# Residual stores on ScalarE's queue, half of the gating product on GpSimd, and the first four MLP units through the common raw ring

## The chip, the cores and the metric

The kernel runs on one core of one Trainium2 chip. The metric is the device time of one launch in microseconds (us), as the median of several runs. Engines are called PE (TensorE, the matrix engine), DVE (VectorE), ACT (ScalarE), POOL (GpSimd) and SP (SyncE, which here only issues transfers).

## The reference

A two-layer backbone over 512 latent tokens and 256 context tokens of width 1024, in float32. Layer 0 mixes tokens by neighbourhood attention beside spatial gating, layer 1 by retention; each layer then has a gated MLP with a depthwise convolution over three tokens. Around every sub-layer stands a sandwich of norms:

```python
x = x + g1 * rmsnorm(y_lat, norm_g[i, 1])
h = modulate(rmsnorm(x, norm_g[i, 2]), sh2, sc2)
x = x + g2 * rmsnorm(conv_ffn(h, ...), norm_g[i, 3])

def conv_ffn(h, w_in, conv_w, conv_b, w_out):
    a = dwconv3(h @ w_in, conv_w, conv_b)      # w_in: 1024 x 5632
    gate, up = jnp.split(a, 2, axis=-1)
    return (jax.nn.silu(gate) * up) @ w_out
```

Layer 0 does this for the latent and the context tokens, layer 1 for the latent tokens alone.

## The kernel before, in words

**Tiles.** Tokens stand in tiles of 128: tiles 0 to 3 are latent, 4 and 5 context. Every matmul is done as three (lines 94, 95, 96) on operands that were split into a high and a low part: ACT copies a 128x1024 unit of weights to its high part (line 68), DVE subtracts that from the raw unit to get the low part (line 69).

**The end of each sub-layer.** Four times in the kernel a mixer or an MLP ends token tile by token tile: after attention (tiles with names ending in b, output `ysg`), after the first MLP (c, `fin` and `yf`), after retention (d, `yr`) and after the last MLP (e, `yf`). For each token tile PE makes the two 512-wide halves of y, DVE adds them up (line 494), and `residual` (from line 316) follows: ACT sums the squares of each half (line 292), DVE multiplies each half by the gate (line 324), POOL makes one over the root mean square in two small instructions (lines 297 and 278), DVE multiplies by it and adds the residual x (line 327), ACT sums squares of the new x, POOL makes its root, the new x is stored to `xd` in DRAM, and the normed x is written in halves by DVE (line 336) and ACT (line 337). There are 6, 6, 4 and 4 such token tiles, 20 in all. In the last of the four the output is stored instead, and the second norm is left out, so `xd` is stored for 16. PE then transposes the normed tiles (line 407 before an MLP, 359 before retention) into the next sub-layer's operand.

**The opening of an MLP.** `plain` (from line 1373) computes the first two features, j = 0 and 1, each from a gate unit (i = 0) and an up unit (i = 1): four units of weights in the order (j, i) = (0,0), (0,1), (1,0), (1,1), called `wp00`, `wp10`, `wp01` and `wp11` in the trace (`wp{i}{j}`; in layer 0 the fourth is `wpm`), loaded as `f{l}{i}{j}r`: `f010r` is layer 0, i = 1, j = 0. Each unit is multiplied first with the operand's first half of columns (`pf`, from the blocks called `hb`), and later, when the last token tiles are through, with the second half (`pf...b`). The later features j = 2 to 21 use another scheme with seven products and are PE's steady work.

**Rings and pools.** Raw units are loaded by SP into a ring of three buffers, `raw`, in a pool that lives through the whole kernel. Up units (i = 1) go to a single buffer of their own, `rawu`, which lies in the MLP's own pool, as do the convolution taps `cw` and some of the split units (in layer 1, all of `wp10`, `wp01`, `wp11`). That pool is opened where the mixer's pool has ended.

**Order.** The code is not run in the order in which it is written: a planner fixes each engine's order when the kernel is built, from its own estimates of durations, the memory that is free and the order of the code. On the chip each engine then goes through its list in that order and waits where an operand is late. All transfers but a few sit on SP's list (line 54).

Of the kernel before, what the change touches and what calls it, by code (L numbers as in the profile page):

```python
# [13 lines left out]
ALU = mybir.AluOpType  # L14
AX = mybir.AxisListType

P = 128
# [23 lines left out]
class Trunk:  # L41
# [274 lines left out]
    def residual(self, t, y, gate, src, last, name, xt):  # L316

        V = self.V
        self.load(xt, src)
        hv = [slice(0, 512), slice(512, 1024)]  # L320
        for n, h in enumerate(hv):
            self.ssq(y[:, h], f"y{name}{t}", n)
        for h in hv:
            V.tensor_tensor(out=y[:, h], in0=y[:, h], in1=gate[:, h], op=ALU.mult)
        r = self.rms(f"y{name}{t}")
        for n, h in enumerate(hv):
            V.scalar_tensor_tensor(out=xt[:, h], in0=y[:, h], scalar=r, in1=xt[:, h], op0=ALU.mult, op1=ALU.add)
            if last:
                self.load(self.out[t * P : (t + 1) * P, h], xt[:, h])
            else:  # L330
                self.ssq(xt[:, h], f"x{name}{t}", n)
        if last:
            return
        self.load(self.xd[t], xt)
        r = self.rms(f"x{name}{t}")
        V.tensor_scalar(out=y[:, hv[0]], in0=xt[:, hv[0]], scalar1=r, scalar2=None, op0=ALU.mult)
        self.S.activation(y[:, hv[1]], xt[:, hv[1]], AF.Copy, scale=r)
# [882 lines left out]
    def ffn(self, l, y, final, gates=None):  # L1220
# [4 lines left out]
        S, V, T, G, a = self.S, self.V, self.T, self.G, self.a  # L1225
# [8 lines left out]
        with ExitStack() as ctx:  # L1234
            fp = self.phase(ctx, f"ffnp{l}", 0)
            cw = fp.tile([P, 44, 4], F32, name=f"cw{l}", tag="cw")
            self.load(cw, a["conv_col"][:, l * 176 : l * 176 + 176])
            if not first:
                for tag in ("rawu", "wh5", "wl5", "wh6", "wl6", "pre0", "pre1"):
                    fp.tile([P, 1024], F32R if tag[0] == "w" else F32, name=f"at{tag}", tag=tag, bufs=1)  # L1240
# [17 lines left out]
            def slot(kind, name):  # L1258

                h = homes[kind][ring[kind] % len(homes[kind])]  # L1260
                ring[kind] += 1
                i = int(h[1])
                if h[0] == "w":
                    pool = self.bp if i < 3 else fp
                    return [pool.tile([P, 1024], F32R, name=f"{name}{x}", tag=f"w{x}{i}", bufs=1) for x in "hl"]
                pool = self.bp if i < 4 else self.lp
                return [pool.tile([P, 1024], F32R, name=f"{name}{x}", tag=f"y{i + m}", bufs=1) for m, x in enumerate("hl")]

            def raw(src, name, up=False):
                if up:  # L1270
                    t = fp.tile([P, 1024], F32, name=f"{name}r", tag="rawu", bufs=1)
                else:
                    t = self.bp.tile([P, 1024], F32, name=f"{name}r", tag="raw", bufs=3)
                self.load(t, src)
                return t

            def win(j, i):
                r = (l * 44 + (j, NF + j)[i]) * P
                return raw(a["ffn_in"][r : r + P], f"f{l}{i}{j}", i == 1)

            H = [slice(0, 512), slice(512, 1024)]
            halves = lambda u: [[x[:, h] for x in u] for h in H]
# [1 line left out]
            def product(ps, w, b, kind):  # L1284


                for k in range(4):
                    self.mm3(
                        ps,
                        [x[:, k * P : (k + 1) * P] for x in w],  # L1290
                        b(k),
                        k == 0 and kind in ("only", "open"),
                        k == 3 and kind != "open",
                        kind == "onto",
                    )
# [4 lines left out]
            def take(pre, i, half, ps, scale=1.0):  # L1300
                for c, b, w in cuts[half]:
                    S.activation(pre[:, i, c : c + w], ps[:, b : b + w], AF.Copy, scale=scale)  # L1302
# [6 lines left out]
            def conv(j, pre):  # L1309
                cv = fp.tile([P, 2, W], F32, name=f"cv{l}{j}", tag="cv", bufs=1)  # L1310
                for i, f in enumerate((j, NF + j)):
                    w0, w1, w2, b = (cw[:, f, m : m + 1] for m in range(4))
                    d, s = cv[:, i, :], pre[:, i, :]
                    S.activation(d, s, AF.Identity, scale=w1, bias=b)  # L1314
                    V.scalar_tensor_tensor(  # L1315
                        out=d[:, 1:W], in0=s[:, 0 : W - 1], scalar=w0, in1=d[:, 1:W], op0=ALU.mult, op1=ALU.add
                    )
                    V.scalar_tensor_tensor(  # L1318
                        out=d[:, 0 : W - 1], in0=s[:, 1:W], scalar=w2, in1=d[:, 0 : W - 1], op0=ALU.mult, op1=ALU.add
                    )  # L1320
                S.activation(cv[:, 0], cv[:, 0], AF.Silu)  # L1321
                V.tensor_tensor(out=cv[:, 0], in0=cv[:, 0], in1=cv[:, 1], op=ALU.mult)  # L1322
                if first and j == NF - 1:
                    g = fp.tile([P, 2, W], F32R, name=f"g{l}{j}", tag="pre0")
                    g = [g[:, 0], g[:, 1]]
                else:
                    g = [fp.tile([P, W], F32R, name=f"g{l}{i}{j}", tag=f"g{i}", bufs=ng) for i in range(2)]
                self.split(g[0], g[1], cv[:, 0])
                return g
# [43 lines left out]
            def plain(js, steps):  # L1373
                d, ps = {}, {}
                for j in js:
                    for i in range(2):
                        if not first and (j, i) == (js[0], 0):
                            u = self.wp
                            ring["o"] += 1
                        elif first and (j, i) == (js[1], 1):  # L1380
                            u = None
                        elif first:
                            u = slot("i", f"wp{i}{j}")
                        else:
                            if (j, i) == (js[1], 1):
                                ring["i"] = 3
                            u = slot("i" if (j, i) == (js[1], 1) else "o", f"wp{i}{j}")
                        if first or u is not self.wp:
                            r = win(j, i)
                            if u is None:  # L1390
                                t = [
                                    fp.tile([P, 2, 512], F32R, name="wpm0", tag="yp"),
                                    self.bp.tile([P, 2, 512], F32R, name="wpm1", tag="G0", bufs=1),
                                ]
                                d[j, i] = [[t[m][:, x] for x in range(2)] for m in range(2)]
                                for m in range(2):
                                    self.split(*d[j, i][m], r[:, H[m]])
                                continue
                            self.split(u[0], u[1], r)
                        d[j, i] = halves(u)  # L1400
                ring["i"] = 0
                self.need(0)
                order = [(j, i) for j in js for i in range(2)]
                for x, (j, i) in enumerate(order):
                    if x == 3:
                        self.need(1)
                    ps[j, i] = [self.ps(f"pf{l}{i}{j}", "A", (P, n))]
                    product(ps[j, i][0], d[j, i][0], hb(11), "open")
                    product(ps[j, i][0], d[j, i][1], hb(21), "close")
                sums = self.block_sums(l)  # L1410
                for j in js:
                    for i in range(2):
                        p = self.ps(f"pf{l}{i}{j}b", "CB"[j], (P, n))
                        ps[j, i].append(p)
                        product(p, d[j, i][0], h12, "open")
                        product(p, d[j, i][1], hb(22), "close")
                        for half in range(2):
                            take(pres[j % len(pres)], i, half, ps[j, i][half])
                    if j == js[0]:
                        steps[0]()  # L1420
                    next(sums, None)
                    gs[j] = conv(j, pres[j % len(pres)])
                    steps[1 + j]()
                for _ in sums:
                    pass
                steps[3]()
# [48 lines left out]
            LAST = NF - 2 * GF  # L1475
            nxt, steps = weights(2)
            plain((0, 1), steps)
            for j in range(2, NF):
                d = nxt
# [45 lines left out]
            if first:  # L1525
# [10 lines left out]
                xt = [fin[:, 4], fin[:, 5], fin[:, 8]]  # L1536
            else:
                fin = fp.tile([P, 4, D], F32, name="fin", tag="blk")
                xt = [fin[:, i] for i in range(4)]
# [193 lines left out]
```

## Time and profile before

| | us |
|---|---|
| median of the runs (1898.76 to 1901.52) | 1898.84 |
| the profiled execution's own time | 1893.99 |
| its span, first to last instruction | 1892.2 |
| PE busy in it | 1800.1 |
| DVE busy | 1402.8 |
| ACT busy | 1029.2 |
| POOL busy | 325.8 |

Rows from the trace give a start in us from the span's beginning, a duration, the engine, the line of the kernel, the operation, and output<-input. What stands in brackets at the end is the idle time of the engine before the row and what ended it. SPq is SP's transfer list. L12 is line 12.

### The profile page before, as it was taken

The numbers are of one execution on the slowest core, as the hardware profiler recorded it, in microseconds if no ns is written. First come the engines' busy times: TensorE is split into PE (matmuls) and PEld (weight loads), VectorE is DVE, ScalarE is ACT, GpSimd is POOL, SyncE is SP. The second block draws the span as 40 slices with busy tenths as digits, with TensorE's granted clock in tenths as the row PEclk, the third lists the DMA queues.
The fourth block names the chain that finished last, engine by engine and source line by source line (L and its number), as shares of the span: only waits on it lengthen the run. The fifth ranks groups of instructions, "written<-read, shape, count | busy, mean of one in ns | idle before, by whom it ended". The sixth has DMA issues, their size and how long they took to land. (4 is left out here: it accounts for less than half of the span.)

```text
span 1892.2 us, 28751 instructions
## 1 busy us (share of the span) xinstructions
PE 1800.1 (95%) x10928; PEld 1591.7 (84%) x10928; DVE 1402.8 (74%) x2352; ACT 1029.2 (54%) x1857; POOL 325.8 (17%) x446
## 2 busy tenths in 40 slices
PE   7998989979999999999989999999999989999998
PEld 4886867669889899998879889988989779889996
DVE  4844788679877778777877666675665689989877
ACT  6533545666555555555565434434444377666763
POOL 1102122130122222222121010011011100222221
PEclk9999999999999999999989999999999989999999
DMA  7333332132577877776744313322421225878772
GB/s 290 115 100 106 93 101 79 57 136 76 175 176 156 184 158 167 145 169 135 232 146 131 119 52 112 112 95 62 134 66 48 100 81 148 212 188 195 178 162 99
DMA packets 83823, 250.32 MB, mean 132 GB/s; under 512 B 10578, under 2 KB 12114, under 8 KB 83684
## 3 DMA queue, kind: packets, MB, share of 16 engines
q1 hardware_dynamic: 58436, 200.72, 32.8%
q0 software_dynamic: 25248, 47.75, 15.2%
q8 instruction: 86, 1.41, 0.3%
q14 instruction: 53, 0.43, 0.1%
HBM read 191.81 MB, written 39.85 MB: 122 GB/s over the span
## 5 line engine op out<-in xcount | busy, mean ns | idle before, releaser
L214 DVE SCALAR_TENSOR_TENSOR acc<-ar,cs,acc 128x512 f32<-128x512 f32 x256 | 189.5, 758 | 35.5 <-DMA ar<-in_adaw 19.7
L1463 POOL DMA_DIRECT2D yf<-yp x64 | 55.9, 873 | 260.2 <-ACT yp L1459 229.2
L1314 ACT ACTIVATE cv<-pre,cw 128x770 f32<-128x770 f32 (+1 forms) x88 | 80.9, 923 | 27.2 <-DVE pre L1307 25.9
L1315 DVE SCALAR_TENSOR_TENSOR cv<-pre,cw,cv 128x769 f32<-128x769 f32 (+1 forms) x88 | 77.2, 880 | 7.2 <-ACT cv L1314 7.2
L1459 ACT COPY yp<-wf 128x512 f32<-128x512 f32 x118 | 67.9, 577 | 18.1 <-PE wf L96 18.0
L1318 DVE SCALAR_TENSOR_TENSOR cv<-pre,cw,cv 128x769 f32<-128x769 f32 (+1 forms) x88 | 77.2, 881 | 0.7
L1302 ACT ACTIVATE pre<-px 128x256 f32<-128x256 f32 (+2 forms) x160 | 54.3, 367 | 41.8 <-PE px L93 33.6
L1098 POOL TENSOR_SCALAR rrr<-rmv 128x2 f32<-128x2 f32 x16 | 3.1, 193 | 363.2 <-DVE rmv L1095 363.2
L1463 POOL DMA_DIRECT2D yd<-ypg x48 | 42.1, 903 | 132.1 <-ACT ypg L1459 130.6
L1463 POOL DMA_DIRECT2D yd<-yp x48 | 42.6, 902 | 126.7 <-ACT yp L1459 126.6
L68 ACT ACTIVATE g<-cv 128x770 fp32r<-128x770 f32 (+1 forms) x44 | 32.5, 738 | 32.6 <-DVE cv L1322 32.4
L93 PE MATMUL px<-hs,wd 128*128 128x384 f32 x240 | 45.4, 337 | 0.0
L93 PEld LDWEIGHTS px<-hs,wd 128*128 128x128 f32 x240 | 42.3, 188 | 1.9 <-DVE pre L1307 0.4
L1307 DVE TENSOR_TENSOR pre<-pre,pz 128x256 f32<-128x256 f32 (+1 forms) x60 | 20.8, 371 | 29.2 <-PE pz L96 29.1
L69 DVE TENSOR_TENSOR g<-cv,g 128x770 fp32r<-128x770 f32 (+1 forms) x44 | 36.1, 821 | 7.4 <-ACT g L68 7.3
L1302 ACT ACTIVATE pre<-py 128x384 f32<-128x384 f32 (+1 forms) x40 | 17.5, 437 | 43.9 <-DVE cv L1318 25.6
L1322 DVE TENSOR_TENSOR cv<-cv 128x770 f32<-128x770 f32 (+1 forms) x44 | 36.2, 822 | 4.3 <-ACT cv L1321 3.1
L1321 ACT ACTIVATE cv<-cv 128x770 f32<-128x770 f32 (+1 forms) x44 | 32.7, 742 | 11.7 <-DVE cv L1318 11.6
L1078 DVE SCALAR_TENSOR_TENSOR of<-rx,e,of 128x256 f32<-128x256 f32 x64 | 28.9, 477 | 8.4 <-PE rx L96 7.9
L869 ACT ACTIVATE sc<-sc,sst 128x512 f32<-128x512 f32 x32 | 23.0, 719 | 22.1 <-DVE sc L860 21.6
L1459 ACT COPY ypg<-wf 128x512 f32<-128x512 f32 x54 | 30.7, 578 | 6.5 <-PE wf L96 6.4
L205 POOL MEMSET acc<- 128x512 f32 x32 | 19.1, 600 | 84.5 <-DVE al L69 62.2
(2985 smaller groups left out, 7181.1 us busy)
## 6 DMA issues: line engine op xcount, KB each, us to landing
ar<-in_adaw SPq DMA_DIRECT2D x96, 512.0 KB
yf<-yp POOLq DMA_DIRECT2D x64, 256.0 KB, 4.2
yd<-yp POOLq DMA_DIRECT2D x54, 256.0 KB, 5.2
yd<-ypg POOLq DMA_DIRECT2D x54, 256.0 KB, 5.0
fin<-xd SPq DMA_DIRECT2D x10, 512.0 KB
xd<-xd SPq DMA_DIRECT2D x8, 512.0 KB
xn<-in_x SPq DMA_DIRECT2D x6, 512.0 KB
xb<-in_x SPq DMA_DIRECT2D x6, 512.0 KB
```

The lines of the kernel that those rows point to most:

```text
L68: self.S.activation(hi, src, AF.Copy)
L69: self.V.tensor_tensor(out=lo, in0=src, in1=hi.bitcast(F32), op=ALU.subtract)
L93: mm = lambda *p, **k: self.nc.tensor.matmul(*p, skip_group_check=True, **k)
L214: V.scalar_tensor_tensor(out=acc[s], in0=raw[:, kk * 512 : kk * 512 + 512], scalar=self.cs[:, 8 * s + k : 8 * s + k + 1], in1=acc[s], op0= ...
L1302: S.activation(pre[:, i, c : c + w], ps[:, b : b + w], AF.Copy, scale=scale)
L1314: S.activation(d, s, AF.Identity, scale=w1, bias=b)
L1315: V.scalar_tensor_tensor(out=d[:, 1:W], in0=s[:, 0 : W - 1], scalar=w0, in1=d[:, 1:W], op0=ALU.mult, op1=ALU.add)
L1318: V.scalar_tensor_tensor(out=d[:, 0 : W - 1], in0=s[:, 1:W], scalar=w2, in1=d[:, 0 : W - 1], op0=ALU.mult, op1=ALU.add)
L1321: S.activation(cv[:, 0], cv[:, 0], AF.Silu)
L1322: V.tensor_tensor(out=cv[:, 0], in0=cv[:, 0], in1=cv[:, 1], op=ALU.mult)
L1459: S.copy(v, ps)
L1463: G.dma_start((yd[t] if first else y[t])[:, o], v, accum_op=ALU.add)
```

## The change

Four edits. In `residual`, the first half of y times gate goes to POOL and only the second half stays on DVE; and the store of the new x to `xd` is issued by ACT instead of SP. In the MLP, the up units of the features j = 0 and 1 are loaded into the common ring `raw` instead of `rawu`, so that all four units of `plain` go through it; and the load of the taps `cw` is moved from the beginning of the MLP to behind the four units.

```diff
@@ residual
-        for h in hv:
-            V.tensor_tensor(out=y[:, h], in0=y[:, h], in1=gate[:, h], op=ALU.mult)
+        for E, h in zip((self.G, V), hv):
+            E.tensor_tensor(out=y[:, h], in0=y[:, h], in1=gate[:, h], op=ALU.mult)
...
-        self.load(self.xd[t], xt)
+        self.S.dma_start(self.xd[t], xt)
@@ ffn
             cw = fp.tile([P, 44, 4], F32, name=f"cw{l}", tag="cw")
-            self.load(cw, a["conv_col"][:, l * 176 : l * 176 + 176])
...
             def win(j, i):
                 r = (l * 44 + (j, NF + j)[i]) * P
-                return raw(a["ffn_in"][r : r + P], f"f{l}{i}{j}", i == 1)
+                return raw(a["ffn_in"][r : r + P], f"f{l}{i}{j}", i == 1 and j > 1)
...
                 ring["i"] = 0
+                self.load(cw, a["conv_col"][:, l * 176 : l * 176 + 176])
                 self.need(0)
```

## Rows read from the trace of the kernel before

**Rows 1.** The page's head: the span, and busy us by engine.

```profile
span 1892.2 us, 28751 instructions
PE 1800.1 (95%) x10928; PEld 1591.7 (84%) x10928; DVE 1402.8 (74%) x2352; ACT 1029.2 (54%) x1857; POOL 325.8 (17%) x446
```

**Rows 2.** Stages: window, its us, busy us (count) of PE, PEld, DVE, ACT, POOL; PEclk.

```profile
409.00:432.50 23.50, 13.96 (x59) 12.09 (x60) 19.82 (x31) 17.31 (x36) 5.67 (x9) 0.72 0.34 117
432.50:460.00 27.50, 27.50 (x157) 27.50 (x157) 25.10 (x31) 16.90 (x28) 0.00 (x0) 0.99 0.20 58
...
500.00:930.00 430.00, 421.61 (x2184) 387.70 (x2183) 342.09 (x488) 246.99 (x425) 101.36 (x131) 1.00 0.74 165
935.00:985.00 50.00, 43.36 (x215) 35.83 (x214) 38.85 (x61) 30.51 (x72) 16.01 (x23) 0.90 0.41 148
...
1522.40:1532.20 9.80, 2.03 (x9) 1.57 (x8) 7.27 (x14) 6.08 (x15) 2.63 (x4) 0.65 0.37 121
1532.20:1560.00 27.80, 27.39 (x214) 26.73 (x215) 24.73 (x40) 19.90 (x37) 0.00 (x0) 0.94 0.25 75
...
1883.00:1892.20 9.20, 0.00 (x0) 0.00 (x0) 3.41 (x6) 1.44 (x4) 1.36 (x2) 0.73 0.26 98
```

**Rows 3.** PE's waits from 408.5 to 434: us in total, times, longest.

```profile
PE ht L407 <- DVE ysg L336: 4.2, 1, 4.2
PE pf L94 <- ACT wp00h L68: 2.2, 1, 2.2
```

**Rows 4.** PE's waits from 1515 to 1540, the longest.

```profile
PE ht L407 <- DVE sb L415: 5.9, 1, 5.9
```

**Rows 5.** Timeline of SP's list between attention and the first MLP.

```profile
420.28 0.33 SPq L54 DMA_DIRECT2D xd<-xb  x1
...
424.38 0.33 SPq L54 DMA_DIRECT2D cw<-in_conv_col  x1
424.75 0.42 SPq L54 DMA_DIRECT2D f010r<-in_ffn_in  x1
```

**Rows 6.** Timeline of ACT and DVE there: splits of the second and third unit.

```profile
410.84 1.04 ACT L68 ACTIVATE wp01h<-f001r 128x1024 fp32r<-128x1024 f32 x1
...
429.55 1.05 ACT L68 ACTIVATE wp10h<-f010r 128x1024 fp32r<-128x1024 f32 x1
...
422.55 1.22 DVE L69 TENSOR_TENSOR wp01l<-f001r,wp01h 128x1024 fp32r<-128x1024 f32 x1
```

**Rows 7.** Timeline of PE there: the first products with `wp10` and with `wp01`.

```profile
432.50 0.52 PE L94 MATMUL pf<-hb,wp10h 128*128 128x384 f32 x1
...
433.13 0.34 PE L94 MATMUL pf<-hb,wp01h 128*128 128x384 f32 x1
```

**Rows 8.** Timelines of SP and ACT between retention and the second MLP.

```profile
1467.27 0.33 SPq L54 DMA_DIRECT2D f101r<-in_ffn_in  x1
...
1528.66 0.43 SPq L54 DMA_DIRECT2D f110r<-in_ffn_in  x1
...
1528.51 1.04 ACT L68 ACTIVATE wp01h<-f101r 128x1024 fp32r<-128x1024 f32 x1
...
1532.49 1.06 ACT L68 ACTIVATE wp10h<-f110r 128x1024 fp32r<-128x1024 f32 x1
```

**Rows 9.** Multiplications of 128x512 by line, and POOL's timeline near 980.

```profile
L324 DVE TENSOR_TENSOR ysg<-ysg,G x12: 680/682/692, 380.1 to 417.4; 128x512 f32<-128x512 f32 x12
...
L955 POOL TENSOR_TENSOR swq<-swq,sin 128x512 f32<-128x512 f32 x8 | 10.4, 1294 | 42.9 <-ACT swq L953 42.9
...
979.27 2.62 POOL L297 TENSOR_SCALAR wyc<-ssyc 128x1 f32<-128x1 f32 x1 [5.48 <-ACT jyc L292]
...
984.90 0.30 POOL L297 TENSOR_SCALAR wxc<-ssxc 128x1 f32<-128x1 f32 x1 [2.36 <-ACT jxc L292]
```

**Rows 10.** Timeline of DVE in the last token tile of the kernel.

```profile
1883.86 0.69 DVE L324 TENSOR_TENSOR yf<-yf,G 128x512 f32<-128x512 f32 x1 [0.85 <-ACT jye L292]
1884.47 0.68 DVE L494 TENSOR_TENSOR yf<-wf1C,yf 128x512 f32<-128x512 f32 x1
```

## The prediction

> **What bounds the kernel now.** The page's head comes first: PE is busy 1800.1 of 1892.2 us [rows 1], so all that PE can win is the 92 us in which it does nothing, and what it loses at a low clock. The second look is at busy time by stage. In the steady part of the first MLP PE has 421.6 of 430 us [rows 2]: nothing that the change touches there can give much. The idle time lies where one sub-layer ends and the next opens. From 409 to 432.5 PE works 13.96 of 23.5 us at a mean granted clock of 0.72, and from 1522.4 to 1532.2 only 2.03 of 9.8 us at 0.65; between the first MLP and retention (935 to 985) it works 43.4 of 50, and the last 9.2 us have no matmul at all [rows 2]. The third look is at what PE waits for there: the normed tile of a late token (4.2 us), the first weight unit's split (2.2) [rows 3], the operand of the last token (5.9) [rows 4]. So in the openings the chain of the last two token tiles sets the pace, and PE has nothing else to do meanwhile. Why not, the timelines show. In layer 0 the third unit `wp01` has its high part from 410.84 and its low part at 423.8 [rows 6], yet PE takes its first product at 433.13, right behind the first product of the second unit `wp10` at 432.50 [rows 7]: PE's list keeps the units in order, and `wp10` is late, for its load was issued at 424.75, right behind the taps at 424.38 [rows 5], and split at 429.55 [rows 6]. In layer 1 the same: `f110r` is issued at 1528.66 and split at 1532.49, while `f101r`, loaded through the common ring at 1467.27, is split at 1528.51 [rows 8]. I read this as the MLP's own pool opening only when the last token's x has been read and stored: all that lives in it (`rawu`, `cw`, layer 1's split units) starts there.
>
> **The change part by part.** The sum is made for the profiled execution, which took 1893.99 us; the median of the runs is 1898.84, and I carry the same difference over to it.
>
> *Units through the common ring, layer 0.* `wp10` no longer waits for the pool: its raw unit is there before 409, its split home lies in the lasting pool, and it can be split right behind `wp00`. With it the order on PE opens up: the first-half products of `wp10` and `wp01`, 24 matmuls each, 48 x 0.175 us (27.5 us / 157 in the stage in which PE is full [rows 2]) = 8.4 us, can move into the 9.5 us in which PE is idle before 432.5. That is the upper end. But each unit needs DVE for 1.22 us [rows 6], and DVE has only 23.5 - 19.82 = 3.7 us free in that stage and 2.4 in the next [rows 2], most of it while it waits for POOL's root in a token's chain. What PE does early it then awaits from DVE, which makes the operands of j = 2. I take half of those 6.1 us: -3.0. Lower end: a subtraction put in front of the last token's chain delays it by its 1.22, so +1.2.
>
> *The same, layer 1.* Here the split home lies in the MLP's pool, so only the landing is saved: `wp10` can be split at 1528.5 where `wp01` was, not at 1532.49 [rows 8]. PE can then begin near 1528.51 + 1.04 = 1529.6 instead of 1532.2: 2.6 us, at most 4.0 (1532.49 - 1528.5). Against that, `f102r` now waits for a buffer of the ring, so the split of `wa2` (1.22 on DVE) falls into a stage with 27.8 - 24.73 = 3.1 us free on DVE [rows 2]. I take -2.0, ends -4.0 and +1.2.
>
> *Taps behind the units.* 0.33 us of SP's list [rows 5] leaves the way of the units; the taps are wanted only when the first convolution starts, behind all four units. Nothing; at worst one late landing in each layer, as long as `f110r` took to its split, 3.8 us [rows 8], if the first convolution had no slack at all.
>
> *Half the gate on POOL.* DVE loses 20 multiplications of 0.682; POOL gets 20 of 1.294 for the same shape [rows 9]. Behind each on POOL stands the small sum of that token's first root, and behind that DVE's next step. The multiplication may start when the first half's squares are summed; the second half's sum takes another 0.85 (the wait in [rows 10]), so where ACT does both in a row POOL is late by 1.294 - 0.85 = 0.44, and where PE delivers the halves further apart by nothing. In the twelve token tiles whose stage leaves DVE room [rows 2] I take +0.3 each, +3.6, with ends 0 and 12 x (0.44 + 0.68) = +13.4, the 0.68 for a collision with DVE. In the four tiles at the crowded openings DVE's 0.682 is worth its length: -2.7, with ends -2.7 and +4.5 by the same 1.12 each. Together +0.9.
>
> On such collisions a row speaks: a POOL instruction that takes 0.30 at 984.90 took 2.62 at 979.27 [rows 9]. The Trainium skill (SBUF — State Buffer, Who interferes with whom) says that a DVE instruction with two SBUF inputs and a GpSimd instruction that reads SBUF exclude each other, the first one holding the port for its whole length; by that rule, the trace agrees, and it gives the slower rival below.
>
> *The stores on ACT's list.* SP's list is freed of 16 issues of 0.33; ACT gets them. 16 x 0.33 = 5.3 us of ACT, upper end if all lay on the path; they fall where ACT waits for POOL's root, so 0. Nothing on SP's list that PE needs stands behind a store any more once the ring feeds the units: lower end, the stores having held back `f010r`, 424.75 - 420.28 = 4.5 us [rows 5], which is already counted above. But behind ACT's two sums of squares the last store goes out up to 1.7 us later (two times 0.85), and the pool opens on it: I take +0.2 at each of two openings, +0.4, ends 0 and 3.4. The Trainium skill (DMA: Bandwidth & Descriptors, Issuing engines are not separate DMA queues) says that issuing from several engines saves only the sequencer's time for the issue. By that rule this edit is worth 0 by itself, against the 4.5 us that the order on SP's list suggests; no row here shows a transfer on ACT's list.
>
> *The end.* DVE's adding of the last half (1884.47) stood behind a gate multiplication that waited 0.85 for ACT [rows 10]; it can go 1.5 us earlier. POOL's multiplication, begun at 1883.8, then ends at 1885.1, against 1886.0 (1884.47 + 0.68 + 0.85) for DVE's second one before: 0.9 at best, less 0.68 in a collision. I take -0.5, ends 0 and -0.9.
>
> Sum: -3.0 - 2.0 + 0.9 + 0.4 - 0.5 = -4.2. The profiled execution would be 1889.8, the median **1894.6**. Differences within 0.2% (3.8 us) are what a measurement of this kernel can't tell from none: faster begins at 1895.0, slower at 1902.6.
>
> **The rivals.**
> (a) PE uses all of the freed order: -8.4 in layer 0, -4.0 in layer 1, the rest as above (+0.8): -11.6, some 1887. For it speaks that PE is idle just where the units were missing, and that its clock stays up when it has work; against it, DVE's 3.7 us.
> (b) DVE takes it back: in both openings PE runs ahead and then waits, as long, for DVE's operands of j = 2. Of the openings 1 us is left of 5: some 1898. For it: DVE is 91% busy from 432.5 to 460 and 89% from 1532.2 to 1560 [rows 2]; against it, PE is full there now, so that DVE is not the later one yet.
> (c) Slower: POOL's multiplication holds up the chain. In a token's chain DVE's list waits for the root before it goes on, so that what POOL is late adds up from tile to tile. At 1.12 (0.44 and a collision) in each of the 16 tiles before another sub-layer this is +17.9, less the openings' 5.0; at half, +9.0 - 5.0 = +4.0, some 1903. It decides from 0.55 us a tile on. For it: POOL's 2.62; against it, where PE sets the pace the second half comes later, and the multiplication is over by then.
> (d) The change doesn't do what it says: the planner, given other times, orders the openings so that `wp10` still comes late, or mixes the steady part anew; then it is some 1898 to 1900.
>
> **How the numbers follow.** Forecast 0.36, (a) 0.24, (b) 0.18, (c) 0.18, (d) 0.04. The forecast's own range is 1891 to 1897, about 0.22 of it faster and 0.14 the same. Faster: 0.22 + 0.24 = 0.46. Same: 0.14 + 0.18 + 0.02 = 0.34. Slower: 0.18 + 0.02 = 0.20. For 8 in 10 the range reaches to (a) at the low end, 1886.5, and half through (c) at the high end, 1903; the far ends of the single bounds (all tiles colliding, all stores on the path) are left out.
>
> **What would show it.** Right: `wp10` split on ACT near 410 in layer 0 and near 1528 on the old scale in layer 1; PE's products with `wp10` and `wp01` well before 432; PE's idle time from attention's last matmul to a full PE down from 9.5 us by some 3, in layer 1 from 7.8 by some 2; `cw` behind the units; POOL rows of 1.3 us at line 324, and the root's first step within 0.5 us of the second sum of squares. Wrong: normed tiles (line 336) further apart than before between the first MLP and retention, long POOL rows, DVE rows at twice their length beside POOL's, or PE waits at j = 2 as long as the idle time that went. The prediction falls if the openings don't shorten, or if the ends of the sub-layers grow by over 4 us in all.

## The result and the profile after

The changed kernel takes 1906.57 us (median of 20 runs) against 1899.52 for the kernel before (20 runs): a ratio of 1.0033, with a 95% interval of 1.0020 to 1.0045. That is 6 us slower (0.0033 x 1900; interval 4 to 9) where 4 us faster was forecast, and beyond the upper end of the range. Five executions in a slower state (2189 to 5387 us) are left out of the ratios of this document. The profiled execution after took 1908.4 us with a span of 1906.2; the two profiles differ by 14.0 us, twice what the medians differ by (7.05), and the profile before came from an execution (1893.99) quicker than any of the 20.

The head of the page after, to be held beside [rows 1]:

```profile
span 1906.2 us, 28736 instructions
PE 1804.8 (95%) x10928; PEld 1596.8 (84%) x10928; DVE 1400.1 (73%) x2332; ACT 1026.9 (54%) x1857; POOL 350.2 (18%) x466
```

POOL got its 20 multiplications and DVE lost them, but DVE's busy time fell by 2.7 us and not by 20 x 0.682 = 13.6: what remains on DVE got longer. The last normed tile of attention's end now comes 10.3 us later (432.4 against 422.1), so the windows that answer to the first two of [rows 2], in the columns given there, are shifted by as much:

```profile
419.30:442.80 23.50, 21.89 (x127) 20.74 (x126) 18.29 (x27) 14.90 (x34) 6.64 (x10) 0.97 0.41 139
442.80:470.30 27.50, 23.45 (x125) 22.75 (x124) 27.12 (x34) 21.54 (x34) 0.00 (x0) 0.91 0.06 20
```

The opening of the first MLP did fill: PE works 21.89 us there where it worked 13.96, at a granted clock of 0.97 instead of 0.72. In the stage behind it PE was full and now loses 4.05 us, in a single wait at the features j = 2 for ACT, which is late in copying out the products called `px` (line 1301):

```profile
466.71 0.69 PE L93 MATMUL px<-hs,wc2h 128*128 128x384 f32 x1 [4.05 <-ACT pre L1301]
```

Both together are still a gain, so the loss must lie elsewhere. The starts of DVE's normed half (line 336) show where, here the first and the last row of the two longest sub-layer ends (duration in ns three times, then the start twice):

```profile
L336 DVE TENSOR_SCALAR ysg<-xb,xb4r x1: 486/486/486, 387.8 to 387.8; 128x512 f32<-128x512 f32 x1
...
L336 DVE TENSOR_SCALAR ysg<-xb,xb3r x1: 486/486/486, 432.4 to 432.4; 128x512 f32<-128x512 f32 x1
L336 DVE TENSOR_SCALAR fin<-fin,xc4r x1: 489/489/489, 951.2 to 951.2; 128x512 f32<-128x512 f32 x1
...
L336 DVE TENSOR_SCALAR yf<-fin,xc3r x1: 486/486/486, 999.6 to 999.6; 128x512 f32<-128x512 f32 x1
```

From the first to the last tile attention's end takes 432.4 - 387.8 = 44.6 us (before 422.1 - 385.5 = 36.6), the first MLP's 48.4 (before 985.9 - 943.4 = 42.5), and the end of retention 25.2 (before 23.3). The three together grow from 102.4 to 118.2 us, by 15.8, and the other stretches of the profiled execution change by +2.3, -2.5, -1.4 and -0.2: together the +14.0 between the two spans.

One token tile of attention's end shows how a tile gets longer (timeline of ACT, POOL and DVE after; columns as in [rows 5 to 7]):

```profile
387.84 0.72 ACT L337 ACTIVATE ysg<-xb,xb4r 128x512 f32<-128x512 f32 x1 [1.08 <-POOL xb4r L278]
387.85 0.49 DVE L336 TENSOR_SCALAR ysg<-xb,xb4r 128x512 f32<-128x512 f32 x1 [1.30 <-POOL xb4r L278]
...
388.47 0.61 ACT L292 ACTIVATE jyb<-ysg 128x512 bf16<-128x512 f32 x1
...
389.09 0.61 ACT L292 ACTIVATE jyb<-ysg 128x512 bf16<-128x512 f32 x1
389.26 1.29 POOL L324 TENSOR_TENSOR ysg<-ysg,G 128x512 f32<-128x512 f32 x1 [1.45 <-ACT jyb L292]
...
389.83 1.28 DVE L324 TENSOR_TENSOR ysg<-ysg,G 128x512 f32<-128x512 f32 x1 [0.90 <-ACT jyb L292]
390.65 0.62 POOL L297 TENSOR_SCALAR wyb<-ssyb 128x1 f32<-128x1 f32 x1
391.35 0.56 POOL L278 TENSOR_TENSOR yb5r<-wyb,mhalf 128x1 f32<-128x1 f32 x1
...
393.46 0.63 ACT L292 ACTIVATE jxb<-xb 128x512 bf16<-128x512 f32 x1
393.50 0.33 ACTq L334 DMA_DIRECT2D xd<-xb  x1
...
395.25 0.72 ACT L337 ACTIVATE ysg<-xb,xb5r 128x512 f32<-128x512 f32 x1 [1.07 <-POOL xb5r L278]
```

Three things are to be seen. ACT does both sums of squares of the next tile (388.47 and 389.09) only behind the normalising of this one (387.84), after an idle 1.08 us. The second sum is complete at 389.80 (389.61 and 0.19 for its reading), but POOL is in its multiplication until 390.55 and begins the root at 390.65, where a free POOL begins it 0.1 after the reading (388.57 after 388.47 in run 1 below). And DVE's multiplication of the other half, which starts inside POOL's, takes 1.28 us where it took 0.68 [rows 9], and the first step of the root beside it 0.62, against 0.30 in the same tile before. The root is late in this way, by 0.69 to 1.31 us, in 15 of the 20 tiles.

### The profile page after: what moved, and what is told of

It reads as the page before. It is cut to its first block, busy times and chain, and to the rows that moved or that the text cites. A ratio compares the mean times of both kernels' runs of the same rounds, so it can differ in the third digit from the quotient of the medians.

```text
span 1906.2 us, 28736 instructions
## 1 busy us (share of the span) xinstructions
PE 1804.8 (95%) x10928; PEld 1596.8 (84%) x10928; DVE 1400.1 (73%) x2332; ACT 1026.9 (54%) x1857; POOL 350.2 (18%) x466
## 5 line engine op out<-in xcount | busy, mean ns | idle before, releaser
L93 PEld LDWEIGHTS px<-hs,wd 128*128 128x128 f32 x240 | 42.4, 188 | 3.9 <-DVE pre L1306 2.3
```

The costliest lines, as they stand in the source:

```text
L93: mm = lambda *p, **k: self.nc.tensor.matmul(*p, skip_group_check=True, **k)
```

## The experiments

Each kernel below was timed beside the kernel before on the same chip; "us" is (ratio - 1) x 1901. The ends are read from the rows of DVE's normed half in each profile (line 336; 335 in run 5), first to last tile, as above: b after attention, c after the first MLP, d after retention, then their sum. The last two columns are the stretch from the last tile of b to the first of c, and from the last tile of d to the end of the span.

| kernel | ratio, 95% interval | us | b, c, d | sum | b to c | d to end |
|---|---|---|---|---|---|---|
| before | | | 36.6, 42.5, 23.3 | 102.4 | 521.3 | 364.7 |
| before, again (9) | 0.9997, 0.9983 to 1.0010 | -0.6 | 37.0, 42.4, 23.3 | 102.7 | 521.1 | 367.7 |
| after | 1.0033, 1.0020 to 1.0045 | +6.3 | 44.6, 48.4, 25.2 | 118.2 | 518.8 | 364.5 |
| half gate only (1) | 1.0032, 1.0015 to 1.0049 | +6.1 | 39.0, 44.1, 23.4 | 106.5 | 521.1 | 366.0 |
| ring and taps only (2) | 0.9937, 0.9915 to 0.9959 | -12.0 | 37.1, 42.5, 22.5 | 102.1 | 514.2 | 364.0 |
| stores only (3) | 1.0048, 1.0031 to 1.0064 | +9.1 | 40.8, 45.7, 24.1 | 110.6 | 521.5 | 367.2 |
| ring and stores (4) | 0.9985, 0.9968 to 1.0002 | -2.9 | 41.2, 46.0, 23.7 | 110.9 | 516.5 | 364.9 |
| ring, stores late (5) | 0.9976, 0.9961 to 0.9991 | -4.6 | 39.1, 46.0, 23.0 | 108.1 | 519.2 | 367.0 |
| ring, sums behind (6) | 0.9979, 0.9966 to 0.9992 | -4.0 | 40.7, 45.4, 23.9 | 110.0 | 519.4 | 364.5 |
| whole gate on POOL (7) | 1.0096, 1.0080 to 1.0112 | +18.2 | 42.5, 46.7, 27.4 | 116.6 | 527.5 | 367.9 |
| ring, layer 0 only (8) | 0.9970, 0.9959 to 0.9982 | -5.7 | 37.2, 42.5, 23.4 | 103.1 | 518.9 | 367.2 |
| ring, layer 1 only (10) | 0.9977, 0.9962 to 0.9991 | -4.4 | 36.6, 42.4, 22.5 | 101.5 | 528.3 | 362.2 |
| ring and half gate (11) | 0.9991, 0.9974 to 1.0007 | -1.7 | 40.0, 42.3, 22.3 | 104.6 | 514.7 | 364.6 |
| ring, taps first (12) | 0.9960, 0.9940 to 0.9980 | -7.6 | 37.5, 42.5, 22.6 | 102.6 | 515.9 | 362.9 |

**The three parts alone.** Theory T1: POOL's multiplication stretches the tiles. Rivals T2 (the new order of PE's list in the MLP's steady part) and T3 (the stores on ACT).

**Run 1.** The half gate alone, on the kernel before:

```diff
-        for h in hv:
-            V.tensor_tensor(out=y[:, h], in0=y[:, h], in1=gate[:, h], op=ALU.mult)
+        for E, h in zip((self.G, V), hv):
+            E.tensor_tensor(out=y[:, h], in0=y[:, h], in1=gate[:, h], op=ALU.mult)
```

> The kernel before with one edit: the first half of the gate multiplication in the residual goes to GpSimd. Theory T1 (the GpSimd multiplication stretches the chain of every token tile): normed tiles (line 336) about 7.4 us apart in layer 0's attention end where they were 6.2 apart; 16 tiles at some 0.5 to 1.1 us each give +8 to +17 us over the kernel before, at least +5. Rival T2 (the new order of TensorE's list in the MLP's steady part is what costs): this kernel keeps that order, so it is within 2 us of the kernel before. Rival T3 (the stores on ScalarE hold up the chains): also within 2 us.

+6.1 us: over T1's least (+5) and under its range (+8 to +17), and not by T1's mechanism alone. The timeline around the first normed tile of this kernel:

```profile
387.07 1.27 POOL L324 TENSOR_TENSOR ysg<-ysg,G 128x512 f32<-128x512 f32 x1
387.14 0.72 ACT L337 ACTIVATE ysg<-xb,xb4r 128x512 f32<-128x512 f32 x1 [0.47 <-POOL xb4r L278]
387.14 1.49 DVE L336 TENSOR_SCALAR ysg<-xb,xb4r 128x512 f32<-128x512 f32 x1 [1.30 <-POOL xb4r L278]
...
388.57 0.30 POOL L297 TENSOR_SCALAR wyb<-ssyb 128x1 f32<-128x1 f32 x1 [0.23 <-ACT jyb L292]
...
393.04 0.72 ACT L337 ACTIVATE ysg<-xb,xb5r 128x512 f32<-128x512 f32 x1 [0.46 <-POOL xb5r L278]
```

The root is not late here: ACT's normalising halves start 5.9 us apart (387.14, 393.04), before 6.05. (It is late, by 0.69 to 1.29 us, in only five of the 20 tiles.) What costs here is DVE's normed half: it starts 0.07 us behind POOL's multiplication, which stood behind the same root in POOL's list, and takes 1.49 instead of 0.49. That happened in 8 of the 16 tiles (1.48 to 1.51 each), and PE's transposes wait for that half. Eight times 1.0 is 8 us at most. The three ends grow by 4.1 us, and the stretch behind PE's last matmul by 0.6 (see the end, below); where the rest of the 6.1 (2.9 to 9.3) arises is not shown.

**Run 2.** The ring and the taps alone, on the kernel before (the third and fourth edit of the change).

> The kernel before with one edit: the first four units of an MLP come through the common raw ring and the taps are loaded behind them; gate and stores as before. T1: the openings' gain is left alone, -2 to -6 us against the kernel before. T2 (the new order in the MLP's steady part costs more than the openings give): +4 to +8 us. T3: as T1, -2 to -6.

-12.0 us (-16.2 to -7.8, from six executions): the fastest of all, and the version to keep. T2 falls: the order behind the opening is changed here too, and the kernel gains. It is not the very order of the changed kernel, but for that one the profiles can be read. From 500 us on PE goes through layer 0's MLP in the same order before, with the ring and after; its first product with `fo06`, well behind that point, stands at (before, ring alone, after):

```profile
617.97 0.39 PE L94 MATMUL wf<-fo06h,g 128*128 128x512 f32 x1
...
613.44 0.39 PE L94 MATMUL wf<-fo06h,g 128*128 128x512 f32 x1
...
622.76 0.39 PE L94 MATMUL wf<-fo06h,g 128*128 128x512 f32 x1
```

From the last normed tile (422.1, 424.4, 432.4) to there it is 195.8, 189.0 and 190.4 us: in the changed kernel, too, opening and steady part together got shorter.

**Run 3.** The stores alone, on the kernel before:

```diff
-        self.load(self.xd[t], xt)
+        self.S.dma_start(self.xd[t], xt)
```

> The kernel before with one edit: the stores of the residual stream are issued by ScalarE instead of SyncE. T1 and T2: within 2 us of the kernel before. T3 (an issue between ScalarE's two sums of squares makes every tile's root late): 0.34 us in each of 20 tiles, +3 to +7 us.

+9.1 us (5.9 to 12.2): T3 is true as well, above its own range. The stores are the larger loss by the medians; the intervals overlap.

**Run 4.** The changed kernel with the gate on DVE again.

> The changed kernel with one part undone: both halves of the gate multiplication on VectorE again; ring, taps and stores as in the changed kernel. T1: 8 to 14 us under the changed kernel, that is some 3 to 6 us under the kernel before. T2: as slow as the changed kernel, +5 to +8 over the kernel before. T3: +2 to +6 over the kernel before.

-2.9 us (-6.1 to +0.4): the ring's -12.0 and the stores' +9.1 add up, closer than their intervals promise. T1 alone asked for -3 to -6, T3 alone for +2 to +6. This kernel also prices the half gate inside the changed one. Its root in the tile shown above:

```profile
389.35 0.79 POOL L297 TENSOR_SCALAR wyb<-ssyb 128x1 f32<-128x1 f32 x1 [2.08 <-ACT jyb L292]
```

The root is not late, but its first step takes 0.79, beside DVE's two multiplications. In the changed kernel it is 0.75 late and takes 0.62: 0.75 - 0.17 = 0.58 us for that tile. The ends grow by 118.2 - 110.9 = 7.3 us over 13 steps, 0.56 a step.

**What a store on ACT costs.** An issue takes 0.33 us, yet the 13 steps between normed tiles grow by 8.8 us (110.9 - 102.1), 0.7 on the mean. The timeline of ACT with the ring alone (2), where the stores are on SP:

```profile
391.55 0.63 ACT L292 ACTIVATE jxb<-xb 128x512 bf16<-128x512 f32 x1
392.09 0.19 ACT L292 ACTIVATION_READ_ACCUMULATOR jxb<-xb 128x1 f32 x1
392.18 0.61 ACT L292 ACTIVATE jyb<-ysg 128x512 bf16<-128x512 f32 x1
392.70 0.18 ACT L292 ACTIVATION_READ_ACCUMULATOR jyb<-ysg 128x1 f32 x1
393.35 0.72 ACT L337 ACTIVATE ysg<-xb,xb5r 128x512 f32<-128x512 f32 x1 [0.46 <-POOL xb5r L278]
393.98 0.61 ACT L292 ACTIVATE jyb<-ysg 128x512 bf16<-128x512 f32 x1
```

And ACT's with ring and stores (4):

```profile
392.33 0.63 ACT L292 ACTIVATE jxb<-xb 128x512 bf16<-128x512 f32 x1
392.37 0.33 ACTq L334 DMA_DIRECT2D xd<-xb  x1
392.87 0.19 ACT L292 ACTIVATION_READ_ACCUMULATOR jxb<-xb 128x1 f32 x1
394.13 0.72 ACT L337 ACTIVATE ysg<-xb,xb5r 128x512 f32<-128x512 f32 x1 [1.07 <-POOL xb5r L278]
394.75 0.62 ACT L292 ACTIVATE jyb<-ysg 128x512 bf16<-128x512 f32 x1
```

While POOL makes the root of x, ACT did the first sum of squares of the next tile (392.18); idle was only the rest, 0.46. With the store in its list the planner puts that sum behind the normalising activation, ACT idles 1.07, and the next tile's root comes a sum later. Theory S1 says that this order costs the time, S2 that the issue and the queue do.

**Run 5.** Ring and taps, the gate on DVE, and the store issued behind the normalising activation, so that the order can stay:

```diff
-        self.S.dma_start(self.xd[t], xt)
...
-        self.S.activation(y[:, hv[1]], xt[:, hv[1]], AF.Copy, scale=r)
+        a = self.S.activation(y[:, hv[1]], xt[:, hv[1]], AF.Copy, scale=r)
+        with self.tc.issue_after(a.ins): self.S.dma_start(self.xd[t], xt)
```

> Units through the common ring and taps behind them, gate on VectorE, and the stores on ScalarE, but issued behind the tile's normalising activation, so that ScalarE's list keeps the next tile's first sum of squares ahead of that activation, as in the kernel before. Theory S1 (the order of ScalarE's list cost the time, not the issue): as the ring alone, -9 to -13 us against the kernel before. Rival S2 (issues of 0.33 us and the transfers of ScalarE's own queue cost it): as ring and stores together, 0 to -4 us.

-4.6 us: missed by S1, and just below S2's best. The first tiles are back at their spacing with the stores on ACT (normed halves at 385.6, 391.6 and 397.7: 6.0 and 6.1 us), so in these two steps issue and queue don't stretch a tile. But the planner changed another place of ACT's list. Its timeline in the fourth tile:

```profile
402.28 0.89 ACT L413 ACTIVATE sa<-ht,ab 128x128 f32<-128x128 f32 x2 [2.38 <-PE ht L407]
...
403.07 0.62 ACT L292 ACTIVATE jxb<-xb 128x512 bf16<-128x512 f32 x1
...
403.68 1.05 ACT L68 ACTIVATE wp00h<-f000r 128x1024 fp32r<-128x1024 f32 x1
404.63 0.61 ACT L292 ACTIVATE jxb<-xb 128x512 bf16<-128x512 f32 x1
```

Two pieces of the operand, which waited for PE, now stand ahead of the tile's sums and a unit's split between them, 0.9 and 1.05 us, and the normed half comes 9.1 us after the one before (ring alone 6.9). At the first MLP's end one step grew from 10.6 to 13.4 us; that one was not taken apart. And the wait for ACT at `px` behind the opening is 3.5 us here (3.7 in run 4), where the ring alone has 0.9.

**Run 6.** The reverse: ring and taps, the gate on DVE, stores on SP, and the order alone forced (a tile's first sums behind the normalising activation of the tile before):

```diff
+        with self.tc.issue_after(self.lastn) if name != "e" and t != 4 and (name, t) != ("d", 0) else ExitStack():
-        for n, h in enumerate(hv):
-            self.ssq(y[:, h], f"y{name}{t}", n)
+            for n, h in enumerate(hv): self.ssq(y[:, h], f"y{name}{t}", n)
...
+        self.lastn = self.S.activation(y[:, hv[1]], xt[:, hv[1]], AF.Copy, scale=r).ins
```

> The same ring and taps, gate on VectorE, stores on SyncE as in the kernel before; only the order of ScalarE's list is forced: each tile's first sums of squares (name jy) are issued behind the normalising activation of the tile before, as the changed kernel has them. S1: some 8 us slower than the ring alone, 0 to -5 us against the kernel before, normed tiles some 0.7 us further apart. S2: as the ring alone, -9 to -13 us.

-4.0 us (-6.5 to -1.5), 8 slower than the ring alone, whose interval it does not touch, and the ends are 110.0 against 110.9 with the stores on ACT: the order alone reproduces the loss, S2 is not needed. The lists of PE, DVE and ACT depart from those of the ring alone only within the three ends, while in run 4 they depart in the openings and behind them too. Its ACT timeline has the same idle time ahead of the normalising (1.07) with no store in the list:

```profile
390.14 0.19 ACT L292 ACTIVATION_READ_ACCUMULATOR jxb<-xb 128x1 f32 x1
391.40 0.72 ACT L337 ACTIVATE ysg<-xb,xb5r 128x512 f32<-128x512 f32 x1 [1.07 <-POOL xb5r L278]
392.03 0.61 ACT L292 ACTIVATE jyb<-ysg 128x512 bf16<-128x512 f32 x1
```

Whether a list with the stores on ACT and no other change of order would cost nothing stays open: no such list was run.

**What POOL costs.** **Run 7.** Both halves of the gate on POOL, on the kernel before (`self.G.tensor_tensor` for both).

> The kernel before with both halves of the gate multiplication on GpSimd. Theory G1 (GpSimd's root waits in the list behind its own multiplication, which delays the whole token chain): a second 1.28 us stands ahead of each root, +1.0 to +1.3 more in each of 16 tiles, +20 to +28 us over the kernel before. Rival G2 (only the collision with VectorE's normalising half costs): VectorE has two multiplications less and collides about as often as with one half, +5 to +10 us.

+18.2 us (15.2 to 21.3): three times the half, a little under G1's range and far above G2's. Nine of its 16 normed halves take over 1 us, against eight with half the gate, so more collisions are not the difference. Its timeline:

```profile
389.46 1.28 POOL L324 TENSOR_TENSOR ysg<-ysg,G 128x512 f32<-128x512 f32 x1 [0.21 <-ACT jyb L292]
...
390.82 0.30 POOL L297 TENSOR_SCALAR wyb<-ssyb 128x1 f32<-128x1 f32 x1
...
391.80 1.42 DVE L327 SCALAR_TENSOR_TENSOR xb<-ysg,yb5r,xb 128x512 f32<-128x512 f32 x2 [1.66 <-POOL yb5r L278]
```

Now the root stands behind a multiplication that may start only when the second sum is read, and DVE waits 1.66 for it. So the first half costs by collision, the second by the wait; the first does both when ACT's order lets its sum come late, as in the changed kernel.

**What each opening gives.** **Run 8.** The ring in layer 0 only (`i == 1 and (l == 1 or j > 1)`), the taps moved in both layers.

> The first four units through the common ring in layer 0 only; layer 1 has its own buffer for the up units as before, taps behind the units in both. If the gain lies in layer 0's opening alone: as the ring alone, -9 to -13 us against the kernel before. If both openings give as the prediction split them, 3 to 2: -5 to -8 us. If layer 1 gives most: -1 to -4 us.

-5.7 us, so layer 0 does not give all.

**Run 9.** The kernel before once more.

> The kernel before, unchanged, as a second profile and as a measure of the noise: every theory expects a ratio whose interval holds 1. If single executions differ in the steady stages, the stretch from the last normed tile of layer 0's attention end to the first of the first MLP's end (521 us in the first profile) differs by some us with the same instructions, while the token tiles' spacing stays within 0.3 us.

No difference. The sums of the ends agree within 0.3 us, while the stretch from the end of the first MLP to that of retention took 518.3 in the first profile and 522.8 in this: one execution can be read to some tenths at the ends and only to some 5 us in the steady stages. The runs 2 and 8 say the same of the b to c stretch: their lists are alike until after c, and it took 514.2 and 518.9.

**Run 10.** The ring in layer 1 only (`i == 1 and (l == 0 or j > 1)`), the taps again moved in both.

> The first four units through the common ring in layer 1 only; in layer 0 the up units keep their own buffer; taps behind the units in both. Theory M (the prediction's mechanism, each opening to its own size): -2 to -4 us against the kernel before, the stretch from the last normed tile after retention to the end 1 to 3 us shorter. Rival N (the ring gives -12 together and layer 0 -5.7, so layer 1 gives the rest): -5 to -8 us.

-4.4 us, between the two expectations; with layer 0's -5.7 it makes -10.1, within the interval of the ring alone (-16.2 to -7.8); the moved taps are in both numbers.

**Run 11.** The changed kernel with the stores on SP again.

> The changed kernel with the stores on SyncE again: ring, taps behind, half of the gate on GpSimd. If the three parts add up (ring -12, half gate +6, stores +9): -4 to -8 us against the kernel before. If GpSimd's multiplication costs more once the openings are free: -3 to +2 us.

-1.7 us (-4.9 to +1.3): ring and gate give less together than apart, and the second expectation fits better. Eight of its 16 normed halves take over 1 us, as in run 1. Against the ring alone the half gate costs 10.3 us here, of which the ends show 2.5 (104.6 against 102.1); where the rest lies was not found.

**Run 12.** The ring without moving the taps.

> The first four units through the common ring, but the taps loaded at the MLP's beginning as before. The prediction put the taps at nothing: as ring and taps together, -7 to -13 us. Rival (the 0.33 us issue and its place ahead of the units is what counts): -4 us or less of a gain.

-7.6 us (-11.4 to -3.8) against -12.0 (-16.2 to -7.8): the ring carries most of it, and whether the taps' place adds something can't be told.

## Why the prediction was wrong, step by step

**Layer 0's opening, -3.0: right in mechanism, too small.** Measured -5.7 (-7.8 to -3.4). The stretch from the last normed tile to the first product with `fo06`, read as in run 2, is 193.2 to 196.6 us in the six profiles without the ring in layer 0 and 186.4 to 190.9 in the eight with it, 6.0 less on the mean. With the ring alone `wp10` is split at 412.59, near the forecast 410, and PE's first products stand at 413.69 and 415.91, against 432.50 and 433.13 in [rows 7] (timelines of ACT and PE):

```profile
412.59 1.04 ACT L68 ACTIVATE wp10h<-f010r 128x1024 fp32r<-128x1024 f32 x1
...
413.69 0.44 PE L94 MATMUL pf<-hb,wp10h 128*128 128x384 f32 x1 [0.33 <-ACT wp10h L68]
...
415.91 0.66 PE L94 MATMUL pf<-hb,wp01h 128*128 128x384 f32 x1 [1.56 <-ACT jxb L292]
```

In the changed kernel the late tiles push the split back to 417.75 and the first product to 421.96, as far ahead of the last normed tile as with the ring alone (10.4 us, 10.7). The halving for DVE was too much: the subtractions did not hold up the last tile's chain (b takes 37.1 with the ring). What PE does early it did await at j = 2, as rival (b) had it, but from ACT: 0.9 us with the ring alone, 4.05 in the changed kernel.

**Layer 1's opening, -2.0: not contradicted.** Measured -4.4 (-7.2 to -1.7), near the far bound of -4.0. With the ring alone `wp10` is split 2.4 us behind the last normed tile (1524.59, 1522.2), before 5.0 (1532.49 in [rows 8], 1527.5). From that tile to PE's first product with `fo15` it is 99.9 to 104.1 us in the six profiles without the ring in layer 1 and 96.9 to 100.9 in the eight with it, 2.2 less on the mean. For the openings as a pair the times (-10.1, -12.0) are nearest to rival (a)'s -12.4; the two means give -8.2, halfway between the forecast's -5.0 and that.

**The taps, 0:** not contradicted.

**Half the gate on POOL, +0.9: wrong.** Measured +6.1. The +0.3 a tile rested on POOL being done before the root is wanted, and the -2.7 on DVE's freed time being worth its length. The collision was priced with the wrong partner: I looked at DVE's other half of the gate, but alone the multiplication meets the normalising half, released by the same root, and adds 1.0 there. Rival (c) named the mechanism of the changed kernel, and its 1.12 a tile is about what the first timeline shows against the kernel before (0.75 that the root starts later, 0.32 that its first step is longer); against ring and stores it is half of that, 0.56 a step. That (c) at half, +4.0, lies near the measured +6.3 is in part luck: it had the stores at nothing and the openings at 5.0.

**The stores on ACT, +0.4: the step that failed most.** "They fall where ACT waits for POOL's root, so 0." Measured +9.1. That wait was not free: the next tile's first sum ran in it, and the new list gave it up. I counted the issues and left out the order that the planner makes of a longer list; rival (d), which had the planner in it, looked at the openings and the steady part, not at the tiles. As an order it costs 0.6 to 0.7 a step between tiles (run 6 and run 4 against the ring alone). By the medians neither of the two would have turned the ring's -12.0 by itself; together they do. The half gate's own size depends on what it stands beside: +6.1 alone, 9.2 with ring and stores (-2.9 to +6.3), of which the ends show 7.3, and 10.3 with the ring alone, of which they show 2.5.

**The end, -0.5: wrong in sign, and small.** The last tile by itself did get shorter: from its first sum to its adding it takes 3.45 us (1898.04 to 1901.49) where it took 4.43 (1883.11 to 1887.54). But it starts later. PE's last matmul, DVE's adding up and the last adding, before and after:

```profile
1882.33 0.68 DVE L494 TENSOR_TENSOR yf<-wf1C,yf 128x512 f32<-128x512 f32 x1
1882.45 0.40 PE L96 MATMUL wf1C<-fo121h,g 128*128 128x512 f32 x1
...
1887.54 1.41 DVE L327 SCALAR_TENSOR_TENSOR fin<-yf,ye3r,fin 128x512 f32<-128x512 f32 x2 [0.85 <-POOL ye3r L278]
...
1895.76 0.40 PE L96 MATMUL wf1C<-fo121h,g 128*128 128x512 f32 x1
...
1897.26 1.28 DVE L494 TENSOR_TENSOR yf<-wf1C,yf 128x512 f32<-128x512 f32 x2
...
1901.49 1.42 DVE L327 SCALAR_TENSOR_TENSOR fin<-yf,ye3r,fin 128x512 f32<-128x512 f32 x2 [0.84 <-POOL ye3r L278]
```

DVE adds up the last tile's halves only behind the adding of the tile before, whose root is 0.75 late behind POOL's multiplication. From the end of the last matmul to that of the last adding it is 6.75 us (1896.16 to 1902.91) where it was 6.10 (1882.85 to 1888.95): 0.65 longer, and as long with the half gate alone (6.73). The step looked at the last tile only and left out that DVE comes to it late.

With the measured sizes the sum is -5.7 - 4.4 + 6.1 + 9.1 = +5.1, against +6.3, or +3.2 with the ring's -12.0; each term is only known to 2 to 4 us. Of the signs that the prediction gave against itself these came: normed tiles further apart, DVE rows at nearly twice their length beside POOL's, ends grown by over 4 us in all, and a wait of PE at j = 2, though not as long as the idle time that went (4.05 against 7.9). Of those for it the root's first step within 0.5 us of the second sum failed: it comes 0.85 behind it in the tile shown.

## What to carry to other kernels

A gap in an engine's list is free only if nothing of the next tile runs in it: before you put an instruction there at no cost, look at what the engine does in that gap, and where a planner orders the list, price the order that comes out and not the instruction. Work moved to a slow engine that also makes the small result the chain waits for is paid twice, as a wait in its list and as a collision with whatever that same result releases on the other engine. Time each part of a change alone: here one part was worth 12 us, hidden under two that cost 15.

## What the hardware showed that was not expected

DVE's scaling of a 128x512 f32 tile, which reads one tile from SBUF, took 1.48 to 1.51 us instead of 0.49 when POOL's multiplication of the same shape had started 0.07 us earlier: it ended 0.29 us after POOL's (388.63 against 388.34), and by 0.28 or 0.29 in all eight tiles of run 1 where this happened. I had reckoned with collisions of DVE instructions with two SBUF inputs only. The Trainium skill (SBUF — State Buffer, Who interferes with whom) says that a `tensor_scalar` may run in a mode that takes both port pairs, and that the one issued first keeps the shared pair for its whole instruction. The trace agrees in that the half never ended before POOL's multiplication; but of its 1.49 us 1.20 lie inside that multiplication and only 0.29 behind it, less than the 0.49 that it takes alone.
